# Two-layer hybrid transformer on one core: order of the second layer's projection, and the context's expert sum on TensorE

## The chip, the cores and the metric

The kernel runs on one NeuronCore of a Trainium2 chip. The metric is the device time of one execution in microseconds (us), as the median of several runs. The engines are called TensorE (PE in the rows; PEld is its loading of weights), VectorE (DVE), ScalarE (ACT), GpSimd (POOL) and SyncE (SP). In this kernel SP and GpSimd issue the transfers.

## The reference, cut to what matters

256 latent tokens and 256 context tokens of width 1024 go through two layers. Only the latents are returned, so layer 1 uses the context's h for keys and values alone.

```python
for l in range(DEPTH):                                     # DEPTH = 2
    with_ctx = l < DEPTH - 1
    mod   = (silu(c) @ w_mod[l] + b_mod[l]).reshape(B, 6, 1, 1024)     # latents
    mod_c = (silu(c_ctx) @ w_mod[l] + b_mod[l]).reshape(6, 1024)       # context
    sh1, sc1, g1, sh2, sc2, g2 = (mod[:, i] for i in range(6))
    sh1c, sc1c, g1c, sh2c, sc2c, g2c = (mod_c[i] for i in range(6))
    h  = _ln(x) * (1 + sc1) + sh1
    hc = _ln(xc) * (1 + sc1c) + sh1c
    pa, pb, pc = split(h @ w_in[l], [P_A, P_A + P_B])
    pa_c, pb_c, pc_c = split(hc @ w_in[l], [P_A, P_A + P_B])
    # three groups of heads: A grouped-query, B neighbourhood, C low-rank;
    # latents attend to latents and context, context to context only
    y = concat([y_gqa, y_na, y_mla]) @ w_out[l]
    x = _ln_affine(ALPHA * x + g1 * y, ln1_g[l], ln1_b[l])
    h = _ln(x) * (1 + sc2) + sh2
    x = _ln_affine(ALPHA * x + g2 * _hier_moe(h, ...), ln2_g[l], ln2_b[l])
    if with_ctx:                                           # layer 0 only
        ...
        xc = _ln_affine(ALPHA * xc + g2c * _hier_moe(hc, ...), ln2_g[l], ln2_b[l])
```

`_hier_moe` chooses one of 4 groups for each token, two of the 8 experts in it, and adds the two experts' outputs with weights.

## The kernel before

Tokens are worked on in four blocks of 128: blocks 0 and 1 are the latents, 2 and 3 the context. On-chip memory is managed by hand: `mem` hands out pieces of 23 units of 128 x 2048 floats, and a new piece waits for the last use of the old one at its place. All large weights come through one list, `stream`, in the order in which it was written; `pump` issues the next load while the pieces loaded and not yet dropped stay under a limit `cap`, whose values towards the end of layer 0 stand in `HC`. Plain loads are issued on SP (L161), loads of experts that are chosen at run time on GpSimd (L142). The order of the instructions on each engine is made by a planner when the kernel is built, from a priority that follows the order of the program; `high_priority` moves a block ahead, and `issue_after` puts an instruction behind another one on its engine. When the kernel runs, each engine serves its instructions in that order.

A matrix product with a large weight is made of three products (L457 to L459): `split` takes a weight apart into a high part (ScalarE, L451) and a low part (VectorE, L452), and the activations are taken apart likewise (L506 and L507).

*End of layer 0.* Passes over the experts end with a loop whose count is known only at run time (L1501); no engine carries work across it. The output rows of most experts lie in DRAM (`ys`). For each block `fetch` gathers the two rows of every token (L1482) into `ACC` and `two`. `fold` scales and adds them, multiplies by the gate g2 and adds the sum to the residual X (L1489 on ScalarE; L1491, L1492, L1493 on VectorE). `combine` adds what the last passes kept on chip, by products with one-hot matrices (L1284), multiplied by g2 (L1293). Then `deepnorm` makes the residual, its norm, and the norm of the next layer (L427 to L438, with L416 and L438 on ScalarE and L419 on GpSimd); here it runs as `second`, called `before` in layer 1.

*Start of layer 1.* `before` runs for the latents with high priority, then `rest_of` folds and combines the context's blocks, with the fold behind the latents' norm on VectorE. `fill(4)` takes four steps of the modulation's product (L320, one weight of 1 MB each). `turned` transposes the normed rows (L489), applies the modulation (L497 on ScalarE and L494 on VectorE for one column of blocks each) and takes the result apart; so h stands in `HT`. The projection follows in the order qa, cq, B chunks 0 and 1 for the latents; then the context's h; then kc (keys of A and the low-rank keys) for all four blocks, B chunks 2 to 4 for all 512 tokens, and v.

In the attention stage that follows, one further step of the modulation's product is put behind each unit of scores.

## Time and profile before

| | |
|---|---|
| median of 3 runs | 1108.3 us (1107.69 to 1109.35) |
| profiled execution | 1106.13 us |
| its span, from the first to the last instruction | 1104.2 us |
| TensorE busy | 994.6 us, 90% of the span |
| VectorE, ScalarE, GpSimd busy | 511.2, 353.1, 302.0 us |
| moved by DMA | 300.54 MB, mean 272 GB/s |

The busy share of an engine is an average over stages with different limits, so the page alone doesn't tell what a change in one stage is worth. Times in the rows count from the start of the span. A row of a timeline gives the start, the time that the merged instructions took, the engine, the line, the operation, the tiles written and read, the count, and in brackets the idle time before it with what ended it. A row of windows gives the stretch, its length, the busy time with the count of instructions of PE, PEld, DVE, ACT and POOL (or of the one engine asked for), the granted clock of TensorE as a share of 2.4 GHz, the busy share of the DMA engines and GB/s. A slice of the page is 27.6 us, a digit its busy share in tenths. An engine with a q behind its name is the engine's sequencer or queue.

### The profile page before, as it was taken

To read this page: it belongs to the slowest core of one execution; us is meant where nothing else is said; L and a number is where in the kernel's file an instruction comes from. 1 tells how busy PE (TensorE), PEld (TensorE's weight loads), DVE (VectorE), ACT (ScalarE), POOL (GpSimd) and SP (SyncE) were. 2 spreads that over 40 slices of the span, in tenths; PEclk is the share of its full clock that TensorE was granted. 3 is DMA by queue.
4 is the path that set the end of the run, shared out by engine and by line. 5 is a ranking of instruction groups with operands and counts; after the bars stand their busy time and mean duration, and the time that the engine had idled before them with its cause. 6 is when DMAs were issued, how large, how long until landed. Compare 5 with 4: busy or idle time off the path is not lost. (4 is left out here: it accounts for less than half of the span.)

```text
span 1104.2 us, 14811 instructions
## 1 busy us (share of the span) xinstructions
PE 994.6 (90%) x5525; PEld 571.6 (52%) x5525; DVE 511.2 (46%) x1364; ACT 353.1 (32%) x712; POOL 302.0 (27%) x325
## 2 busy tenths in 40 slices
PE   4999999999999999999985479999998899999894
PEld 2788745457866454444332259844466554433231
DVE  5643357775577210100013887266666654242244
ACT  4533155563552111111112365144444222111111
POOL 2111133350001432343341222042300145344420
PEclk9999999999999999999998789999997899999997
DMA  9812157610269999999998653435425799999992
GB/s 374 321 64 88 48 191 278 218 44 34 107 259 390 399 423 422 363 414 421 423 421 352 249 202 112 173 137 193 150 78 230 306 387 423 421 421 421 420 421 90
DMA packets 46207, 300.54 MB, mean 272 GB/s; under 512 B 5394, under 2 KB 5778, under 8 KB 14388
## 3 DMA queue, kind: packets, MB, share of 16 engines
q0 software_dynamic: 25824, 177.81, 39.2%
q1 hardware_dynamic: 20308, 121.75, 29.4%
q8 instruction: 45, 0.74, 0.3%
q14 instruction: 30, 0.25, 0.1%
HBM read 292.19 MB, written 7.34 MB: 271 GB/s over the span
## 5 line engine op out<-in xcount | busy, mean ns | idle before, releaser
L142 POOL DMA_INDIRECT u<-in_w_exp,u x162 | 161.1, 994 | 307.4 <-PE psa L1204 95.9
L1204 PE MATMUL psa<-u,u 128*32 128x512 f32 (+2 forms) x1040 | 212.9, 596 | 8.1 <-DMA u<-in_w_exp,u 8.1
L458 PE MATMUL psa<-u,u 128*128 128x512 f32 (+3 forms) x400 | 140.0, 351 | 2.2 <-DVE u L452 2.2
L457 PE MATMUL psa<-u,u 128*128 128x512 f32 (+3 forms) x400 | 140.8, 356 | 0.9 <-ACT u L506 0.7
L459 PE MATMUL psa<-u,u 128*128 128x512 f32 (+3 forms) x400 | 139.1, 351 | 0.1
L1204 PEld LDWEIGHTS psa<-u,u 128*32 128x32 f32 (+2 forms) x1040 | 64.6, 126 | 132.5 <-issue 109.1
L1191 PEld LDWEIGHTS psc<-u,u 128*128 128x128 f32 x640 | 83.0, 197 | 33.2 <-issue 29.0
L1191 PE MATMUL psc<-u,u 128*128 128x256 f32 x640 | 93.7, 297 | 3.0 <-DVE u L1177 2.1
L889 POOL TENSOR_SCALAR u<-u,ri 128x512 f32<-128x512 f32 (+1 forms) x48 | 68.4, 1430 | 99.1 <-DVE ri L887 81.5
L1211 DVE TENSOR_TENSOR scr<-scr,psa 128x256 f32<-128x256 f32 x26 | 10.9, 421 | 163.4 <-ACT scr L1210 157.7
L458 PEld LDWEIGHTS psa<-u,u 128*128 128x128 f32 x400 | 76.1, 190 | 12.9 <-DVE u L452 4.3
L457 PEld LDWEIGHTS psa<-u,u 128*128 128x128 f32 x400 | 75.5, 190 | 12.2 <-ACT u L506 1.1
L459 PEld LDWEIGHTS psa<-u,u 128*128 128x128 f32 x400 | 75.4, 190 | 9.3 <-issue 0.9
L886 ACT ACTIVATE u<-psa,nm 128x512 f32<-128x512 f32 (+1 forms) x96 | 58.4, 615 | 54.7 <-DVE nm L884 49.8
L1262 PE MATMUL pse<-u,scr 128*64 128x512 f32 (+1 forms) x288 | 70.4, 599 | 0.8 <-DMA u<-in_w_exp,u 0.8
L452 DVE TENSOR_TENSOR u<-u,u 128x1024 fp32r<-128x1024 f32 (+4 forms) x38 | 56.1, 1486 | 19.5 <-ACT u L451 19.4
L1210 ACT ACTIVATE scr<-psa 128x256 f32<-128x256 f32 x26 | 10.0, 385 | 171.5 <-PE psa L1204 171.5
L1193 ACT ACTIVATE u<-psc 128x512 f32<-128x512 f32 x52 | 31.1, 597 | 101.5 <-PE psc L1191 58.9
L884 DVE TENSOR_REDUCE nm<-psa 128x1 f32<-128x512 f32 (+1 forms) x80 | 53.1, 683 | 13.1 <-PE psa L874 9.5
L419 POOL TENSOR_TENSOR lns<-lns,mhalf 128x1 f32<-128x1 f32 x22 | 14.2, 648 | 162.7 <-DVE lns L418 130.3
L1249 PE MATMUL pse<-u,scr 128*32 128x512 f32 (+2 forms) x232 | 57.3, 600 | 1.4 <-ACT scr L1239 1.4
L451 ACT ACTIVATE u<-u 128x1024 fp32r<-128x1024 f32 (+4 forms) x38 | 47.4, 1266 | 16.2 <-PE psa L458 3.5
(317 smaller groups left out, 1366.5 us busy)
## 6 DMA issues: line engine op xcount, KB each, us to landing
u<-in_w_mod SPq DMA_DIRECT2D x48, 1024.0 KB, 6.5
u<-in_w_exp SPq DMA_DIRECT2D x30, 1024.0 KB, 6.9
u<-in_w_out SPq DMA_DIRECT2D x8, 1024.0 KB, 4.8
ys<-u SPq DMA_DIRECT2D x12, 512.0 KB, 8.2
u<-in_w_in_b SPq DMA_DIRECT2D x10, 512.0 KB, 11.7
u<-in_w_in_v SPq DMA_DIRECT2D x4, 960.0 KB, 5.9
u<-in_w_in_qa SPq DMA_DIRECT2D x4, 768.0 KB, 11.7
u<-in_ln_rows SPq DMA_DIRECT2D x6, 512.0 KB, 7.1
```

Source lines behind the costliest of these rows:

```text
L142: G.indirect_dma_start(out=b.ap(UNIT), out_offset=None, in_=wexp_rows, in_offset=bass.IndirectOffsetOnAxis(ap=idx, axis=0), bounds_check=N ...
L452: V.tensor_tensor(l_[:, c], w[:, c], h[:, c].bitcast(F32), OP.subtract)
L457: PE.matmul(p, lhsT=a[0], rhs=b[0], start=first, stop=False)
L458: PE.matmul(p, lhsT=a[0], rhs=b[1], start=False, stop=False)
L459: PE.matmul(p, lhsT=a[1], rhs=b[0], start=False, stop=final)
L884: V.tensor_reduce(out=nm[:, s, 0:n], in_=pv, axis=AX.X, op=OP.max, negate=True)
L886: S.activation(P[:, i, :], pv[:, i, :], AF.Exp, bias=nm[:, s, i:i + 1], accum_out=su[:, s, i:i + 1])
L889: (G if s == 0 else V).tensor_scalar(P[:, i, :], P[:, i, :], ri[:, s, i:i + 1], None, op0=OP.mult)
L1191: PE.matmul(pv[:, j, :], lhsT=H[b][:, k * 128:(k + 1) * 128], rhs=OH[:, b, :], start=(b == 0 and i == 0), stop=(b == nb - 1 and i == 1))
L1204: PE.matmul(g[r, :], lhsT=XG[:, k, at * 128 + r.start:at * 128 + r.stop], rhs=W(t, k // 4).v(4, 512)[:, k % 4, :], start=(k == 0), stop=(k ...
L1249: PE.matmul(y[r, :], lhsT=hc[:, c * 128 + r.start:c * 128 + r.stop], rhs=W(t, 2).v(2, D)[:, c, f * 512:f * 512 + 512], start=(c == 0), sto ...
L1262: PE.matmul(y[r, :], lhsT=hc[:, c * 128 + r.start:c * 128 + r.stop], rhs=W(t, 2).v(2, D)[:, c, f * 512:f * 512 + 512], start=(c == 0), sto ...
```

## The change

In layer 1, the list of loads, the filler steps and the projection are put in another order; kc is multiplied for the latents first and for the context later, with the parts of its weight kept in between (`keep`); B chunks 2 to 4 are multiplied in two halves of 256 tokens, with their weights kept likewise (`at`, `kept`). The limit on loaded pieces becomes 3 units once the latents' h is made (`HC[4]`).

In layer 0, the fold of the two context blocks is left out. Four diagonal matrices are made from the identity and the tokens' weights (`diag`), and `combine` adds the products of these with the gathered rows to the same sum on TensorE, in plain f32. The sum is copied by ScalarE, and the multiplication by g2 is done later in `second`, on VectorE behind the last part of the latents' h (`lowest`), where the norm then adds it to the residual.

```diff
-HC = (8, 7, 3, 5)
+HC = (8, 7, 3, 5, 3)
...
-    for k in ("qa", "cq"):
-        for c in range(2):
-            stream_chunk(k, 1, c)
+    for c in range(2):
+        stream_chunk("qa", 1, c)
+    stream_mod(1, 1, 0, 2)
+    for c in range(2):
+        stream_chunk("cq", 1, c)
     for c in range(2):
         stream_b(1, c)
-    stream_mod(1, 1, 0, 4)
     for c in range(2):
         stream_chunk("kc", 1, c)
     for c in range(2, 5):
         stream_b(1, c)
-    stream_mod(1, 1, 4, 8)
+    stream_mod(1, 1, 2, 4)
     for c in range(2):
         stream_chunk("v", 1, c)
+    stream_mod(1, 1, 4, 8)
...
-            V.tensor_tensor(lo, wv, hi.bitcast(F32), OP.subtract)
+            lowest.append(V.tensor_tensor(lo, wv, hi.bitcast(F32), OP.subtract).ins)
...
-        def chunk(k, blocks):
+        def chunk(k, blocks, keep=False):
...
-                pre.pop((k, c))
+                if not keep:
+                    pre.pop((k, c))
...
-        def p_b(c):
+        def p_b(c, at=None):
...
+            if c in kept:
+                w = kept.pop(c)
+            else:
+                w = split(take(("inb", l, c)), 1024)
+                drop(("inb", l, c))
+                pump()
+            if at == 0:
+                kept[c] = w
             n = 256 if (last and c < 2) else 512
+            ts = slice(0, n) if at is None else slice(256 * at, 256 * at + 256)
...
-                three(p[:, 0:n], [x[:, j, :] for x in wv], hpart(j, slice(0, n)), j == 0, j == 7)
+                three(p[:, ts], [x[:, j, :] for x in wv], hpart(j, ts), j == 0, j == 7)
...
             rest_of()
+            fill(2)
             for c in range(2):
                 presplit("qa", c)
             make_h()
-            fill(4)
             for j in range(0, 8, 2):
                 turned([(j, 0), (j + 1, 0)])
             for b in range(2):
                 xn[b].free()
+            pump(HC[4])
             together(*[before(b, xn) for b in range(2, 4)])
             p_qa()
             p_cq()
             for c in range(2):
                 p_b(c)
+            p_kc(chunk("kc", lat, True))
+            for c in range(2, 5):
+                p_b(c, 0)
+                fill(c > 2)
             for j in range(0, 8, 2):
                 turned([(j, 1), (j + 1, 1)])
...
-            p_kc(chunk("kc", every))
+            p_kc(chunk("kc", range(2, 4)))
             for c in range(2, 5):
-                p_b(c)
+                p_b(c, 1)
             p_v()
...
+                    if final and not last and b > 1:
+                        pairs += [(diag.v(2, 2, 128)[:, b - 2, j, :], r[:, fs]) for j, r in
+                                  enumerate((ACC[b], two[b].v(D)))]
...
+                    elif final and b > 1:
+                        S.activation(ACC[b][:, fs], p, AF.Copy)
...
+        diag = None if last else mem.get(512)
...
             fetch(range(2, nb))
+            for b in range(2):
+                for j in range(2):
+                    S.activation(diag.v(2, 2, 128)[:, b, j, :], ident, AF.Copy, scale=sc_[:, b + 2, 2 + j:3 + j])
...
         def second(b, xn):
             xn[b] = mem.get(D) if last else acc[b]
+            if not last and b > 1:
+                with tc.issue_after(lowest[-1]):
+                    V.tensor_tensor(ACC[b], ACC[b], BC["g2", 1], OP.mult)
...
             if not last:
-                with tc.issue_after(normed[-1]):
-                    fold(range(2, nb))
                 combine(fin, range(2, nb), True)
+                for x in two[2:] + [diag]:
+                    x.free()
```

## Rows read from the trace of the kernel before

**Rows 1.** Page, 40 slices of the span: busy tenths of TensorE:

```profile
PE   4999999999999999999985479999998899999894
```

**Rows 2.** Busy times by windows, whose columns are told in the section above:

```profile
604.00:642.60 38.60, 19.31 (x80) 10.40 (x81) 33.04 (x64) 15.90 (x23) 10.07 (x12) 0.69 0.62 214
...
677.00:722.50 45.50, 45.50 (x238) 39.35 (x237) 14.86 (x48) 10.13 (x26) 5.03 (x8) 1.00 0.31 112
...
722.50:860.00 137.50, 125.15 (x619) 70.87 (x616) 89.57 (x221) 63.91 (x132) 33.24 (x30) 0.93 0.47 166
...
900.00:1060.00 160.00, 152.79 (x850) 62.23 (x848) 57.51 (x118) 25.70 (x48) 67.26 (x68) 1.00 1.01 418
```

**Rows 3.** TensorE's waits, 604 to 690 us: line, releaser, total, times, longest:

```profile
PE pse L320 <- DMA u<-in_w_mod: 7.3, 2, 7.0
...
PE psc L680 <- DVE scr L609: 2.0, 1, 2.0
```

**Rows 4.** Timeline of TensorE between the two layers:

```profile
615.94 1.05 PE L320 MATMUL pse<-u,csil 128*32 128x512 f32 x2
...
629.52 1.54 PE L489 MATMUL psc<-ident,u 128*128 128x128 f32 x6 [1.40 <-ACT u L438]
...
638.03 3.64 PE L320 MATMUL pse<-u,csil 128*32 128x512 f32 x16 [6.97 <-DMA u<-in_w_mod]
...
641.61 1.25 PE L489 MATMUL psc<-ident,u 128*128 128x128 f32 x8
...
642.61 0.42 PE L457 MATMUL psa<-u,u 128*128 128x384 f32 x1
```

**Rows 5.** ScalarE's timeline of the same stretch:

```profile
612.96 1.15 ACT L1489 ACTIVATE u<-u,sc__2337 128x1024 f32<-128x1024 f32 x1 [5.39 <-DMA u<-ys,find]
...
615.62 1.15 ACT L1489 ACTIVATE u<-u,sc__2337 128x1024 f32<-128x1024 f32 x1 [1.51 <-DMA u<-ys,find]
...
616.68 1.13 ACT L416 ACTIVATE scr<-u,lns 128x1024 bf16<-128x1024 f32 x1
...
630.46 1.21 ACT L497 ACTIVATE scr<-psc,modT 128x256 f32<-128x256 f32 x2 [0.99 <-PE psc L489]
```

**Rows 6.** VectorE's timeline of the same stretch:

```profile
611.93 0.15 DVE L415 TENSOR_SCALAR lns<-dns 128x1 f32<-128x1 f32 x1
...
628.04 2.48 DVE L1491 SCALAR_TENSOR_TENSOR u<-u,sc__2337,u 128x1024 f32<-128x1024 f32 x2
...
630.43 2.36 DVE L1492 TENSOR_TENSOR u<-u,u 128x1024 f32<-128x1024 f32 x2
...
637.37 0.99 DVE L494 TENSOR_SCALAR scr<-psc,modT 128x256 f32<-128x256 f32 x2
...
639.41 1.30 DVE L507 TENSOR_TENSOR u<-scr,u 128x512 fp32r<-128x512 f32 x2
```

**Rows 7.** SP's timeline: issues of weight loads:

```profile
588.45 0.81 SPq L161 DMA_DIRECT2D u<-in_w_in_cq  x2
...
603.91 10.40 SPq L161 DMA_DIRECT2D u<-in_w_mod  x3
...
630.55 0.33 SPq L161 DMA_DIRECT2D u<-in_w_mod  x1
```

**Rows 8.** Last of eight gathers (L1482) on GpSimd; landing times of all:

```profile
608.01 1.33 POOL L1482 DMA_INDIRECT u<-ys,find  x1 [0.30 <-issue]
...
DMA to landing us min/median/max: 7.5/18.4/25.2
```

**Rows 9.** Windows of TensorE alone: matmuls of 256 columns, then 512:

```profile
674.70:684.17 9.47, 9.47 (x81) 1.00 0.01 2
...
684.94:689.97 5.03, 5.03 (x23) 1.00 0.00 0
```

**Rows 10.** Timeline of TensorE: a filler step, f32 products of 128x512:

```profile
651.75 1.06 PE L320 MATMUL pse<-u,csil 128*32 128x512 f32 x8 [0.34 <-DMA u<-in_w_mod]
...
726.23 2.88 PE L811 MATMUL psa<-u,u 128*128 128x512 f32 x6
```

More of the change, by code (lines that the diff above doesn't have):

```diff
@@ L419, in moments @@
         G.tensor_tensor(rs[:, 2:3], rs[:, 1:2], mhalf[:, 0:1], OP.pow)
-    normed = []
+    lowest = []
     def deepnorm(x, h, gain, bias, last=False, alpha=ALPHA, total=None, eps=EPS):
@@ L436, in deepnorm @@
                 yield
-            normed.append(V.tensor_tensor(rs[:, 0:1], rs[:, 3:4], rs[:, 2:3], OP.mult).ins)
+            V.tensor_tensor(rs[:, 0:1], rs[:, 3:4], rs[:, 2:3], OP.mult)
             S.activation(h, x, AF.Identity, bias=rs[:, 0:1], scale=rs[:, 2:3])
@@ L551, in chunk @@
                 for x in w:
-                    x.free()
+                    if not keep:
+                        x.free()
         def lead(k):
@@ L684, in p_qa @@
                 defer(turn)
-        def p_b(c):
+        kept = {}
+        def p_b(c, at=None):
             if c == 0:
@@ L691, in p_b @@
                     K.extend(x.v(n) for x in k)
-            w = split(take(("inb", l, c)), 1024)
-            drop(("inb", l, c))
-            pump()
+            if c in kept:
[6 more added lines that the diff above has]
+                kept[c] = w
             n = 256 if (last and c < 2) else 512
+            ts = slice(0, n) if at is None else slice(256 * at, 256 * at + 256)
             wv = [x.v(8, 128) for x in w]
@@ L698, in p_b @@
             for j in range(8):
-                three(p[:, 0:n], [x[:, j, :] for x in wv], hpart(j, slice(0, n)), j == 0, j == 7)
+                three(p[:, ts], [x[:, j, :] for x in wv], hpart(j, ts), j == 0, j == 7)
             if c < 2:
-                S.activation(QB[c][:, 0:n], p[:, 0:n], AF.Copy, scale=0.125)
+                S.activation(QB[c][:, ts], p[:, ts], AF.Copy, scale=0.125)
             elif c < 4:
-                S.activation(KB[c - 2], p, AF.Copy)
+                S.activation(KB[c - 2][:, ts], p[:, ts], AF.Copy)
             else:
-                S.activation(QB[2][0:64, :], p[0:64, 0:nq], AF.Copy, scale=0.125)
-                V.tensor_copy(KB[2][0:64, :], p[64:128, :])
-            for x in w:
-                x.free()
+                if at != 1:
+                    S.activation(QB[2][0:64, :], p[0:64, 0:nq], AF.Copy, scale=0.125)
+                V.tensor_copy(KB[2][0:64, ts], p[64:128, ts])
+            if at != 0:
+                for x in w:
+                    x.free()
             tick()
@@ L1592, in rest_of @@
             if not last:
-                with tc.issue_after(normed[-1]):
-                    fold(range(2, nb))
                 combine(fin, range(2, nb), True)
+                for x in two[2:] + [diag]:
+                    x.free()
             for k in list(split_y.values()) + oht:
```

## The prediction

> **What bounds the kernel now.** I read the page's slices first [rows 1]. TensorE is close to full nearly everywhere. The one deep dip inside the span lies at the 22nd to 24th digit, where layer 0 hands over to layer 1, and there the edits lie. Next come busy times by stage [rows 2]. From 604.0 to 642.6 us TensorE works 19.3 of 38.6 us. The rest of the projection (677.0 to 722.5) is wholly busy, the attention stage behind it is at 125 of 137.5 us, and the last long stage (900 to 1060) moves 418 GB/s at full DMA share. Its expert loads depend on the routing of layer 1 and on memory that attention gives back, so time saved before 720 should arrive at the end. What remains is the handover, and there the list of waits [rows 3] and the four timelines [rows 4 to 7] must be read side by side.
>
> The timeline of TensorE [rows 4] shows it empty from 617.0 (615.94 + 1.05) until the latents' normalised rows come (L489, for the second block at 629.52), then waiting 7.0 us for a weight of the modulation (L320 at 638.03, rows 3). That step ran at half speed: 16 matmuls in 3.64 us, where eight take 1.06 us at 2.4 GHz [rows 4, 10]. The projection starts at 642.61. Three different things hold it back.
> First, ScalarE. It serves its instructions in order. Two scalings of the context's expert rows (L1489) sit in front of the latents' L416 and wait for their gathers until 612.96 and 615.62 [rows 5]. The input of L416 was there at 611.93 + 0.15 = 612.1 [rows 6], yet it starts at 616.68: 4.6 us of a serial chain.
> Second, VectorE. From 628.04 to 637.37 it folds the context's rows (two instructions each of L1491, L1492, L1493, then four of L1293; the first two groups stand in rows 6). L494, which the latents' transposed h needs, comes behind them, although ScalarE's half (L497) began at 630.46 [rows 5].
> Third, SP. The fourth modulation weight is issued only at 630.55 [rows 7], and TensorE, also in order, stands before it until 638.03.
>
> **The change part by part.** The fold goes away and its sum goes to TensorE, the filler steps ahead of the latents' h shrink from four to two, and work that needs only latents moves ahead of the context's h.
>
> *ScalarE's fold out of the chain.* Without L1489 the first L416 can start at 612.1. The four small scalings of the identity wait for no DMA. Gain 4.6 us; the second block's L489 moves from 629.5 to about 624.9.
>
> *VectorE's fold and the two filler steps out of the way.* L494 then follows L497, in the old run's times at about 631.1, instead of 637.37: 6.3 us. In the old run another context sum (1.1 us) stood between L494 and L507, and L320 and the second group of transposes stood before the projection until 642.61 [rows 4, 6]. The new wait after the last L507 keeps the context's product behind all of the latents' h; what queues behind it on VectorE is only the context's own chain. In the old run's times L507 would end and the projection start at about 633.9, so 8.7 us earlier. The low bound is the 6.3 us alone. With the first part: start at 642.6 - 4.6 - 8.7 = 629.3.
>
> *Diagonal products on TensorE.* For two blocks, two halves and two operands there are eight f32 products of 128x512, each two instructions, so 16. The nearest row is L811: six such instructions in 2.8 us, 0.47 each [rows 10]; 16 take 7.5 us. They need the gathers. The last is issued at 608.0, and the quickest of the eight landed 7.5 us after its issue [rows 8]: 615.5. I take 7.5 and not the median of 18.4, because most of the eight were issued into the expert stream, and this one has no expert load behind the loop in front of it. The old work of this place ended at 617.0, so TensorE is done at 624.5, just before the L489 that can start at 624.9. I put 0.4 us on it, bounds 0 and 3.1.
>
> *The clock.* The granted clock over 604 to 642.6 was 0.69 [rows 2]. Old: the filler steps took the slow start and lost 3.64 - 2.1 = 1.5 us. New: the projection may take it. TensorE will have been idle for a shorter time, as the products fill it until 624.5. Bounds 0 and 1.5, I take 0.8.
>
> *Two filler steps moved later.* Eight instructions are one step, 1.06 us [rows 10]. Two steps now lie in a stretch where TensorE is full: +2.1 us.
>
> *B chunks in two halves.* Three chunks of 24 matmuls of 512 columns become 144 of 256. Of matmuls with 512 columns 22 begin in 5.03 us, 0.2286 each, and of those with 256 columns 79 in 9.47 us, 0.120 each [rows 9] (one and two in the counts had begun before). So 17.3 - 16.5 = +0.8 us. The keys are already multiplied block by block; splitting them by block adds nothing to TensorE, and their weights are split once and kept.
>
> *VectorE behind the start.* Two products of the context (2.36 us for two of this shape, as L1492 in rows 6) and its first sum (1.24, half of L1491's pair) now come after the latents' h and ahead of the split of the second projection weight. TensorE would wait up to 3.6 us for it; or the old wait for L609 (2.0 us, rows 3) disappears because VectorE has 9.7 us less of folding. Bounds -2.0 and +3.6, I take +1.5. That the context's h comes later costs nothing, as TensorE has the latents' keys (48 x 0.12 = 5.8 us) and half of the B chunks (8.6) to do first; without that cover up to 14 us of TensorE time would lie open. ScalarE's four copies out of PSUM take about 0.6 us each, like L497, and lie beside it.
>
> *The loads.* Two weights of the modulation now come ahead of cq, and the rest come later. Before the loop one of 1 MB takes the place of three pieces of 0.5 MB; I cost this at nothing, since SP's issues after 603.9 [rows 7] give cq about 20 us until it is needed.
>
> Sum: -4.6 - 8.7 + 0.4 + 0.8 + 2.1 + 0.8 + 1.5 = -7.7 us. On the profiled execution, 1106.1 us with a span of 1104.2, that is 1098.4. That execution lies 2.2 us under the median of 1108.3, so the forecast for the median is 1100.6.
>
> **Rivals.** *Copies in ScalarE's queue.* The new copies of the context's sums wait for the products, until about 624.5. If they stand ahead of the latents' L438, ScalarE again blocks the chain as L1489 did, and the first 4.6 us are lost: -3.1, so 1105.2. For it: exactly this happened in rows 5. Against: they now come behind two more steps, and the latents' chain has the higher priority.
> *The modulation weight still late.* The change moves the wait and doesn't remove it: the two later filler steps stand in TensorE's queue between the B chunks, and their weights are loaded only under the smaller limit on loaded pieces, three units. The price is the 7.0 us of rows 3 once more: -0.7, so 1107.6. Against: the step lies some 25 us behind the start.
> *Gathers late, slower than before.* TensorE now waits for the gathers in front of the latents' transposes; before, only the folds did. About 3 us lie between landing and need. Each further us is a us lost; a landing 10.7 us late (at 626) eats the gain, and over 13 us late makes it slower than now by more than can be told from no change. The largest landing time of the eight is 25.2 us [rows 8]: 633.2, 17.7 us late, which gives -7.7 + 17.7 - 3 = +7.0, so 1115.3. It decides where SP's longer list of loads starts at 603.9 beside them. Against it: in the old run three weights of 1 MB were issued from 603.9 on as well, and that gather came in 7.5 us.
> The Trainium skill (DMA: Bandwidth & Descriptors, "Queues, rings and completion order") says that each DMA engine takes turns, packet by packet, between the queue rows that have work. By that rule a longer list on SP's queue does not put the gathers further back; only expert loads ahead of them in their own queue would, and by it this rival gives no more than the forecast's time. The fast landing after the loop agrees, 7.5 us against the largest of 25.2 us; no run yet shows the longer list.
>
> **How the numbers follow.** Forecast 0.62, copies 0.14, late weight 0.12, late gathers 0.12. A measurement of this kernel can tell about 0.2%, 2.2 us, from no change. Faster: 0.62 + 0.14 = 0.76; same: 0.12; slower: 0.12. The predicted time is the forecast's, 1100.6. With every open bound on its good side (0 for the products and the clock, -2.0 for VectorE) it is -12.4, about 1096; I set the low end at 1095.5. The high end takes in the late weight, 1108.0; beyond it lie the late gathers.
>
> **What would show it.** Right: no L1489 for the context; the first L416 by 613; L494 within a us of its L497; the projection's first matmul between 628 and 632, no wait of 7 us for a modulation weight; the end of the projection some 7 us earlier than 722.5, and the stages behind it as long as before. The products' step is wrong if TensorE waits long for the gathers before L489; VectorE's if waits for L452 or L609 of more than 4 us stand in the projection; the cover if TensorE waits before the context's transposes. The prediction as a whole is wrong if the projection starts early and attention or the last DMA stage takes the gain back.

## The result, and the profile after

The changed kernel takes 1114.9 us, the median of 7 runs (1113.5 to 1119.3), against 1108.2 us for the kernel before in runs beside it. The ratio is 1.0066 with a 95% interval of 1.0050 to 1.0082: about 7 us slower. The forecast was 1100.6 in a range that ended at 1108.0. The profiled execution took 1114.92 us with a span of 1113.1, against 1106.13 and 1104.2. Two stray executions (1966.5 us of `e7_keys_only` below, 2458.3 us of the kernel before beside e5 to e8) are left out of every ratio and of e7's median.

Lines moved with the edit. In the changed kernel `split` is L453 (ScalarE) and L454 (VectorE), the products of the projection L459 to L461, the filler step L322, the norm's L416 to L440 stand two lines lower than before, the transposes are L491, the modulation L499 and L496, `combine` L1306, ScalarE's new copies of the context's sums L1315, and the context's product with g2 L1616. The heads' norm and rotation (L603 to L609 before) are L607 to L613.

Busy times by stage of the changed kernel, with the columns of [rows 2]: handover from the first product of `combine` to the first matmul of the projection, projection, attention to its last values, and from there to the ranks of the routing:

```profile
605.50:638.20 32.70, 24.27 (x77) 13.13 (x77) 20.96 (x56) 14.14 (x23) 9.98 (x12) 0.82 0.62 227
638.20:727.80 89.60, 84.31 (x541) 76.92 (x540) 50.32 (x116) 38.28 (x75) 15.33 (x16) 0.93 0.39 139
727.80:817.70 89.90, 86.58 (x457) 39.78 (x456) 58.64 (x137) 43.13 (x102) 30.94 (x26) 1.00 0.50 172
817.70:867.90 50.20, 40.04 (x170) 31.14 (x169) 30.92 (x81) 20.93 (x31) 2.21 (x4) 0.77 0.48 183
```

The same four stages of the kernel before:

```profile
604.50:642.60 38.10, 19.28 (x80) 10.38 (x81) 32.83 (x62) 15.73 (x23) 10.07 (x12) 0.69 0.62 217
642.60:722.80 80.20, 77.06 (x464) 67.22 (x463) 43.98 (x114) 35.92 (x71) 14.92 (x16) 1.00 0.45 164
722.80:811.70 88.90, 85.63 (x444) 39.79 (x442) 58.26 (x137) 43.85 (x102) 31.03 (x26) 1.00 0.46 157
811.70:859.40 47.70, 38.96 (x172) 30.71 (x171) 30.95 (x81) 20.06 (x31) 2.21 (x4) 0.80 0.47 181
```

The handover became 5.4 us shorter. The projection behind it became 9.4 us longer, attention 1.0 and the stage behind it 2.5. What remains to the end of the span is 245 us in both. So two questions stand: why the handover gained 5.4 us and not 13.3 (642.6 to 629.3), and what makes the projection longer.

**The handover.** ScalarE's timeline of the changed kernel:

```profile
614.85 1.15 ACT L418 ACTIVATE scr<-u,lns 128x1024 bf16<-128x1024 f32 x1 [7.86 <-DVE lns L417]
...
623.12 0.60 ACT L1315 ACTIVATE u<-psa 128x512 f32<-128x512 f32 x1 [7.02 <-PE psa L1306]
624.83 0.60 ACT L1315 ACTIVATE u<-psa 128x512 f32<-128x512 f32 x1 [1.12 <-PE psa L1306]
625.33 1.14 ACT L418 ACTIVATE scr<-u,lns 128x1024 bf16<-128x1024 f32 x1
```

VectorE's timeline of the same stretch (the two L417 give the inputs of the two L418):

```profile
607.03 0.09 DVE L1437 MEMSET capv<- 128x2 f32 x2 [2.08 <-ACT u L453]
607.06 1.23 DVE L1518 TENSOR_TENSOR u<-u,u 128x1024 f32<-128x1024 f32 x1
...
614.67 0.15 DVE L417 TENSOR_SCALAR lns<-dns 128x1 f32<-128x1 f32 x1
...
618.39 0.15 DVE L417 TENSOR_SCALAR lns<-dns 128x1 f32<-128x1 f32 x1
...
636.82 1.18 DVE L496 TENSOR_SCALAR scr<-psc,modT 128x256 f32<-128x256 f32 x2 [0.35 <-ACT scr L499]
...
642.19 2.35 DVE L1616 TENSOR_TENSOR u<-u,u 128x1024 f32<-128x1024 f32 x2
```

And TensorE's timeline:

```profile
615.14 1.06 PE L322 MATMUL pse<-u,csil 128*32 128x512 f32 x6
619.52 10.56 PE L1306 MATMUL psa<-u,u 128*128 128x512 f32 x24 [3.33 <-DMA u<-ys,find]
634.06 0.69 PE L491 MATMUL psc<-ident,u 128*128 128x128 f32 x2 [3.98 <-ACT u L440]
...
638.18 0.67 PE L459 MATMUL psa<-u,u 128*128 128x384 f32 x1
```

The first L418 starts the moment its input is there. The second block's input is there at 618.5 and L418 starts at 625.33: 6.8 us behind two copies that wait for the products. This is the first rival of the prediction, in the trace. The products themselves wait 3.3 us for the gathers and then take 10.6 us, until 630.1 and not 624.5. VectorE's step came as predicted: L496 starts as soon as ScalarE's L499 releases its buffer, after 0.35 us of waiting (in [rows 6] it stood behind the fold), and no wait for a modulation weight is left in front of the projection.

**The projection.** TensorE's waits, 604 to 728 us, in the columns of [rows 3]:

```profile
...
PE psa L460 <- DVE u L454: 2.8, 2, 1.8
PE psa L459 <- DVE scr L607: 1.4, 1, 1.4
PE psa L461 <- DVE u L454: 1.1, 1, 1.1
...
```

The first of the splits that it waits for, of the second projection weight (cq), on VectorE:

```profile
649.46 1.22 DVE L454 TENSOR_TENSOR u<-u,u 128x1024 fp32r<-128x1024 f32 x1
```

Windows inside the projection (the fourth column from the right is POOL's, then the granted clock):

```profile
638.20:643.00 4.80, 4.80 (x18) 4.72 (x17) 4.34 (x7) 2.80 (x5) 0.00 (x0) 0.50 0.00 0
...
652.00:656.60 4.60, 2.75 (x23) 2.55 (x22) 3.75 (x13) 4.45 (x7) 2.55 (x2) 1.00 0.01 2
656.60:660.00 3.40, 3.40 (x19) 3.38 (x17) 2.27 (x8) 1.69 (x3) 2.05 (x3) 0.54 0.00 0
660.00:664.00 4.00, 1.51 (x8) 0.92 (x7) 3.13 (x7) 2.10 (x4) 0.84 (x2) 0.93 0.74 262
664.00:666.90 2.90, 2.90 (x15) 2.90 (x15) 2.46 (x6) 1.42 (x3) 1.93 (x1) 0.50 0.02 6
```

TensorE now begins the projection before cq is split. The context's product (L1616), its sums and its norm stand in VectorE's queue in front of these splits (L454), and TensorE waits for them. It was idle 5.3 us (89.60 - 84.31) instead of 3.1. Three stretches run at half clock, 1.2 GHz: 638.2 to 643, 656.6 to 660, 664 to 666.9, together some 5.4 us of work lost (half of 4.8, 46% of 3.4, half of 2.9). TensorE had waited ahead of each of them, but a gap alone does not decide it: behind the wait of 0.95 us at 650.7 the clock stayed at 1.00, and the projection before was at 1.00 throughout with a wait of 2.0 us in it (L680, [rows 3]).

### The profile page after: what moved, and what is told of

Same layout as the page of the kernel before. It is cut to its first block, busy times and chain, and to the rows that moved or that the text cites. A ratio compares the mean times of both kernels' runs of the same rounds, so it can differ in the third digit from the quotient of the medians.

```text
span 1113.1 us, 14992 instructions
## 1 busy us (share of the span) xinstructions
PE 1008.9 (91%) x5613; PEld 587.9 (53%) x5613; DVE 506.3 (45%) x1357; ACT 354.8 (32%) x720; POOL 303.5 (27%) x325
## 5 line engine op out<-in xcount | busy, mean ns | idle before, releaser
L459 PE MATMUL psa<-u,u 128*128 128x256 f32 (+3 forms) x424 | 149.0, 354 | 4.0 <-ACT u L453 1.7
L460 PE MATMUL psa<-u,u 128*128 128x256 f32 (+3 forms) x424 | 147.2, 348 | 4.7 <-DVE u L454 4.7
L461 PE MATMUL psa<-u,u 128*128 128x256 f32 (+3 forms) x424 | 145.5, 347 | 1.2 <-DVE u L454 1.1
L459 PEld LDWEIGHTS psa<-u,u 128*128 128x128 f32 x424 | 83.1, 197 | 16.3 <-ACT u L453 3.4
L460 PEld LDWEIGHTS psa<-u,u 128*128 128x128 f32 x424 | 83.4, 197 | 13.6 <-DVE u L454 5.8
L461 PEld LDWEIGHTS psa<-u,u 128*128 128x128 f32 x424 | 82.5, 196 | 9.8 <-DVE u L454 1.4
L1281 PE MATMUL pse<-u,scr 128*64 128x512 f32 (+1 forms) x288 | 67.2, 600 | 1.0 <-DMA u<-in_w_exp,u 0.6
L454 DVE TENSOR_TENSOR u<-u,u 128x1024 fp32r<-128x1024 f32 (+4 forms) x38 | 56.3, 1486 | 23.3 <-ACT u L453 23.0
L1306 PE MATMUL psa<-u,u 128*128 128x512 f32 x144 | 48.4, 470 | 11.9 <-DVEq L1526 4.5
```

The costliest lines, as they stand in the source:

```text
L454: V.tensor_tensor(l_[:, c], w[:, c], h[:, c].bitcast(F32), OP.subtract)
L459: PE.matmul(p, lhsT=a[0], rhs=b[0], start=first, stop=False)
L460: PE.matmul(p, lhsT=a[0], rhs=b[1], start=False, stop=False)
L461: PE.matmul(p, lhsT=a[1], rhs=b[0], start=False, stop=final)
L1281: PE.matmul(y[r, :], lhsT=hc[:, c * 128 + r.start:c * 128 + r.stop], rhs=W(t, 2).v(2, D)[:, c, f * 512:f * 512 + 512], start=(c == 0), sto ...
```

## The experiments

Two theories stood at the start. A: the copies in ScalarE's queue hold the chain, as in rival 1, and without them the change pays. B: the sum on TensorE pays, and the new order (loads, filler steps, projection) costs. One table holds all runs: each ratio is against runs of the kernel before beside it, and 0.001 is 1.1 us. The stages are those of the windows above, from one profiled execution each, cut at the same instructions. They leave out what lies ahead of `combine`, whose first product began at 604.5 us before, at 605.5 in the changed kernel, and anywhere from 604.3 to 609.1 in the others (e1 at 608.3 and e9 at 604.3, which differ up to there in the list of loads alone). So the stages of one execution do not add up to a ratio.

| kernel | median, us | ratio, 95% interval | handover | projection | attention | to the ranks |
|---|---|---|---|---|---|---|
| before | 1108.2 | 1 | 38.1 | 80.2 | 88.9 | 47.7 |
| after | 1114.92 | 1.0066 [1.0050, 1.0082] | 32.7 | 89.6 | 89.9 | 50.2 |
| e1_sum_only | 1098.47 | 0.9914 [0.9891, 0.9936] | 30.0 | 81.5 | 87.0 | 46.2 |
| e2_order_only | 1114.34 | 1.0056 [1.0034, 1.0078] | 39.1 | 82.9 | 89.9 | 49.3 |
| e3_copies_behind | 1117.25 | 1.0079 [1.0054, 1.0103] | 36.1 | 88.7 | 89.9 | 50.3 |
| e4_diag_late | 1108.73 | 1.0005 [0.9988, 1.0021] | 33.4 | 84.5 | 89.9 | 46.1 |
| e5_copies_diag | 1111.19 | 1.0016 [1.0002, 1.0029] | 31.4 | 87.2 | 89.9 | 49.4 |
| e6_sum_copies | 1098.82 | 0.9904 [0.9882, 0.9926] | 28.5 | 82.1 | 86.9 | 49.3 |
| e7_keys_only | 1107.94 | 0.9987 [0.9974, 1.0000] | 30.0 | 91.8 | 85.7 | 46.1 |
| e8_loads_only | 1106.35 | 0.9976 [0.9964, 0.9988] | 31.7 | 82.8 | 89.4 | 46.2 |
| e9_steps_only | 1101.69 | 0.9952 [0.9933, 0.9970] | 29.5 | 81.9 | 88.9 | 47.7 |
| e10_whole_chunks | 1112.78 | 1.0049 [1.0033, 1.0066] | 33.4 | 89.7 | 88.9 | 47.6 |
| e11_steps_early | 1111.25 | 1.0035 [1.0019, 1.0051] | 35.0 | 85.5 | 88.9 | 47.7 |
| e12_split_behind | 1106.70 | 0.9983 [0.9964, 1.0001] | 29.6 | 85.8 | 89.9 | 49.4 |

A difference of two kernels below is the difference of their ratios times 1108 us, with the intervals' half widths added as squares (the root of their sum).

### The two halves of the change, each alone

`e1_sum_only` is the kernel before with the context's sum on TensorE (`diag` allocated where it is first used), and nothing of the order:

```diff
-                with tc.issue_after(normed[-1]):
-                    fold(range(2, nb))
                 combine(fin, range(2, nb), True)
+                for x in two[2:] + [diag]:
+                    x.free()
```

with the edits of `combine`, `second` and the diagonal matrices as in the change.

> The kernel before with the context's sum on TensorE alone (diag allocated at its first use); loads, filler steps and projection as before. Theory A (the copies out of PSUM in ScalarE's queue hold up the latents' chain, the order of the projection is sound): the latents' last norm ends at about 634, not 629.5, but L494 no longer waits for a fold and TensorE waits for the modulation weight until 638 as before, so the projection starts at 642 to 644: 1108 to 1110 us. Theory B (the new order of loads and projection is what costs, the sum gains): the projection starts by 640 and the time is 1104 to 1107 us.

`e2_order_only` is the reverse: `HC`, the list of loads, `fill`, `keep` and `at` as in the change; `rest_of` stays as it was:

```diff
             if not last:
                 with tc.issue_after(normed[-1]):
                     fold(range(2, nb))
                 combine(fin, range(2, nb), True)
```

> The changed kernel with the old fold of the context on ScalarE and VectorE; loads, filler steps and projection in the new order. Theory A: the latents' norm ends at 629 to 631 as before, L494 waits for the fold until 637, and without two filler steps the projection starts at 639 to 641; waits behind it as in the changed kernel, so 1107 to 1111 us. Theory B: the waits for splits and the half clock in the projection (some 8 us) come with the order, 1112 to 1116 us.

Measured: the sum alone gains 9.5 us, a ratio of 0.9914, and is the fastest form so far; the order alone loses 6.2. Theory B has the direction; e1 is better than either theory expected. The time of e2 lies in B's range, but B's mechanism does not show there: its projection is only 2.7 us longer than before, with 0.5 us of waiting for a split and a clock of 0.98, so the waits and the half clock of the changed kernel's projection did not come with the order alone. The handover of e1, 30.0 us, is 8.1 shorter than before, and its projection stays at full clock:

```profile
608.30:638.30 30.00, 26.12 (x95) 13.71 (x96) 21.68 (x56) 15.80 (x26) 10.09 (x12) 0.85 0.77 278
638.30:719.80 81.50, 77.96 (x465) 67.48 (x464) 48.38 (x113) 35.50 (x71) 15.33 (x16) 1.00 0.43 160
```

Against [rows 2] TensorE has 26 us of work in the handover instead of 19: the products, and still four filler steps (32 instructions). The granted clock over the handover is 0.85 instead of 0.69, and the projection starts at full clock.

### The copies, and what stands behind them

`e3_copies_behind` is the changed kernel with the copies behind the latents' last normalisation:

```diff
-            S.activation(h, x, AF.Identity, bias=rs[:, 0:1], scale=rs[:, 2:3])
+            normed.append(S.activation(h, x, AF.Identity, bias=rs[:, 0:1], scale=rs[:, 2:3]).ins)
...
-                        S.activation(ACC[b][:, fs], p, AF.Copy)
+                        with tc.issue_after(normed[-1]):
+                            S.activation(ACC[b][:, fs], p, AF.Copy)
```

> The changed kernel with the four copies out of PSUM put behind the latents' last norm activation on ScalarE. Theory A: the first L418 of the second block starts at about 618.5 instead of 625.3; the norm ends 6 us earlier, and then the products on TensorE, until 630, hold the transposes: the projection starts at 633 to 635, and the time falls by 3 to 5 us to 1110 to 1112. Theory B: the projection starts earlier but waits for splits and loads instead, 1114 to 1116 us.

Measured: 1117.25, no gain. ScalarE's timeline of e3 says why:

```profile
622.12 1.15 ACT L418 ACTIVATE u<-u,lns 128x1024 f32<-128x1024 f32 x1 [1.72 <-DVE lns L417]
...
632.31 1.67 ACT L453 ACTIVATE u<-u 128x512 fp32r<-128x512 f32 x3 [8.95 <-PE psa L1306]
633.89 1.13 ACT L418 ACTIVATE u<-u,lns 128x1024 f32<-128x1024 f32 x1
```

Another instruction took the copies' place: the split of the second piece of qa's weight, whose memory the products give back. It waits 8.95 us for them, and block 1's L418 stands behind it.

`e4_diag_late` is the changed kernel with `diag` allocated where it is first used, so that the last passes run without its quarter of a unit being held:

```diff
         two = []
-        diag = None if last else mem.get(512)
...
             fetch(range(2, nb))
+            diag = mem.get(512)
```

> The changed kernel with the piece for the diagonal matrices taken at its first use instead of ahead of the passes. If this piece, by moving others in memory, costs only the wait for g2 in the last passes (7.8 us of TensorE's wait, given back to 1.0 us at the loop): 1113.5 to 1114.5 us, cq loaded at 625 as now. If the placement also makes the loads of cq late (issued at 624.8 and 630.1), these move to about 606 and the time falls by 3 to 6 us, 1109 to 1112.

`e5_copies_diag` has both edits, that of e3 and that of e4.

> The changed kernel with two edits together: the diagonal's piece is taken at first use (as in e4_diag_late), and ScalarE's copies of the context's sums stand behind the latents' last normalisation. Theory A (the copies in ScalarE's queue cost the latents' chain some 4 us, once no other wait stands there): 1104 to 1106, 3 to 5 us under e4_diag_late. Theory B (the copies are not what ends last, or the split of the first weight waits for the products in their place, as in e3_copies_behind): 1108 to 1111, with the second L453 behind a wait for L1306 of several us.

Measured: `diag` taken late gains 6.8 us (+-2.5) against the changed kernel, and 7.0 (+-3.1) with the copies moved (e5 against e3). The allocation of one quarter unit was no part of the prediction at all. Neither expectation for e4 came as told: cq was still issued late (626.1 and 631.4 us), and yet the time fell just below both ranges. Moving the copies again brings nothing, e5 against e4 +1.2 (+-2.4). VectorE's timeline of e5:

```profile
626.81 0.16 DVE L439 TENSOR_TENSOR lns<-lns 128x1 f32<-128x1 f32 x1 [0.32 <-POOL lns L421]
631.59 1.90 DVE L454 TENSOR_TENSOR u<-u,u 128x512 fp32r<-128x512 f32 x3 [4.61 <-PE psa L1306]
...
634.21 0.16 DVE L439 TENSOR_TENSOR lns<-lns 128x1 f32<-128x1 f32 x1 [0.62 <-POOL lns L421]
```

ScalarE's half of the split now found other memory, VectorE's half did not: 4.6 us of waiting for the products, ahead of block 1's L439. `e12_split_behind` is e5 with these three pieces behind that L439:

```diff
-            V.tensor_tensor(l_[:, c], w[:, c], h[:, c].bitcast(F32), OP.subtract)
+            with tc.issue_after(behind) if behind else nullcontext():
+                V.tensor_tensor(l_[:, c], w[:, c], h[:, c].bitcast(F32), OP.subtract)
```

where `behind` is the latents' last L439 for qa's second piece, and nothing otherwise.

> e5_copies_diag with VectorE's three split pieces of the first weight's second chunk put behind the latents' last L439. In e5_copies_diag these pieces waited 4.61 us for the products L1306, and block 1's L439 stood behind them until 634.21. If that in-order wait is what holds the handover: L439 by 630, the projection 3 to 4 us earlier against the start of combine (27.5 to 28.5 us instead of 31.4), 1106 to 1108. If the projection's first 25 us go at the pace of VectorE and an earlier start is given back there: the start moves and the projection grows by as much, 1109.5 to 1112.

Measured: 1106.7, and e12 is 3.7 us (+-2.5) faster than e5. The lines of e12 that answer to those of e5 (L440 and L456 here):

```profile
628.11 0.16 DVE L440 TENSOR_TENSOR lns<-lns 128x1 f32<-128x1 f32 x1 [0.66 <-POOL lns L422]
630.71 1.90 DVE L456 TENSOR_TENSOR u<-u,u 128x512 fp32r<-128x512 f32 x3 [2.44 <-PE psa L1309]
```

So the in-order wait was real, and it stood in three places one after the other: ScalarE's copies, ScalarE's split, VectorE's split. Only with the last of them gone does the time move, by 1 to 6 us against e5. Against e4, where none of the three was touched, e12 gains 2.4 us (+-2.7), which can't be told from nothing. Even then e12 stays 7.6 us (+-3.2) behind e1, so the queues are not the main loss.

`e6_sum_copies` is e1 with the copies behind the latents' last normalisation, by the edit of e3:

```diff
-                        S.activation(ACC[b][:, fs], p, AF.Copy)
+                        with tc.issue_after(normed[-1]):
+                            S.activation(ACC[b][:, fs], p, AF.Copy)
```

> e1_sum_only (the context's sum on TensorE, all else as before) with the copies behind the latents' last normalisation on ScalarE. In e1_sum_only all six split pieces of the first weight ran at 608.3, ahead of the products, so no split can wait for them; the second block's L416 had its input at 619.7 and started at 623.85 behind the copies. Theory A: 4 us off the chain, projection start 26 to 27 us after the start of combine instead of 30, 1094 to 1096. Rival (TensorE's filler steps or VectorE end as late as the chain did): 1097 to 1100, no difference to e1_sum_only.

Measured: as e1 (-1.1 +-3.5). ScalarE's timeline of e6:

```profile
628.02 1.24 ACT L438 ACTIVATE u<-u,lns 128x1024 f32<-128x1024 f32 x1 [0.85 <-DVE lns L437]
629.17 2.04 ACT L1297 ACTIVATE u<-psa 128x512 f32<-128x512 f32 x4
631.08 1.04 ACT L497 ACTIVATE scr<-psc,modT 128x256 f32<-128x256 f32 x2
```

The chain up to L438 became shorter, but the four copies now stand in front of L497, 2.0 us, and the projection's start moved 1.5 us against the start of `combine`. In the medians it can't be told from nothing. Theory A fell as a cause of the result: the waits are there, the price is small.

### What in the new order costs

Four kernels take the order apart, all with the sum on TensorE and `diag` taken late. `e7_keys_only` adds to e1 the latents' keys ahead of the context's h:

```diff
             for c in range(2):
                 p_b(c)
+            p_kc(chunk("kc", lat, True))
             for j in range(0, 8, 2):
                 turned([(j, 1), (j + 1, 1)])
...
-            p_kc(chunk("kc", every))
+            p_kc(chunk("kc", range(2, 4)))
```

> e1_sum_only plus one part of the new order of the projection: the keys (kc) are multiplied for the latents ahead of the context's h, with the weight's parts kept; the list of loads, the filler steps and the whole B chunks stay as before. If the order of the loads and filler steps costs the 10 us between e1_sum_only and e4_diag_late: 1097 to 1100. If the order of the projection costs them: 1103 to 1108.

`e8_loads_only` adds to e1 the change's list of loads, `pump(HC[4])`, `fill(2)` ahead of the latents' h and `fill(c > 2)` behind the whole B chunks:

```diff
             rest_of()
+            fill(2)
...
             make_h()
-            fill(4)
...
+            pump(HC[4])
             together(*[before(b, xn) for b in range(2, 4)])
...
                 p_b(c)
+                fill(c > 2)
```

> e1_sum_only plus the new list of loads, the limit of three units and the filler steps in their new places (two ahead of the latents' h, two behind B chunks 3 and 4), with the old order of the projection. If the loads and filler steps cost the 10 us between e1_sum_only and e4_diag_late: 1103 to 1108, with a wait of TensorE for a modulation weight or for cq, and two more steps behind the scores. If the order of the projection costs them: 1097 to 1101.

`e9_steps_only` moves only the steps and their weights:

```diff
-    stream_mod(1, 1, 0, 4)
+    stream_mod(1, 1, 0, 2)
...
+    stream_mod(1, 1, 2, 4)
     for c in range(2):
         stream_chunk("v", 1, c)
+    stream_mod(1, 1, 4, 8)
...
-            fill(4)
+            fill(2)
...
                 p_b(c)
+                fill(c > 2)
```

> e1_sum_only with two of the four filler steps taken out of the stretch ahead of the projection and put behind B chunks 3 and 4, and their two weights of the modulation put behind the B chunks in the list; the rest of the list, the limits and the order of the projection stay as before. If the place of the steps makes most of the 8 us between e1_sum_only and e8_loads_only: 1103 to 1106, with a wait for the modulation's weight behind the B chunks and some 2 us more in the attention stage. If the longer list ahead of cq and the limit of three units make it: 1098 to 1101.

`e10_whole_chunks` is e4 with the B chunks 2 to 4 whole again, behind the context's h:

```diff
-            for c in range(2, 5):
-                p_b(c, 0)
-                fill(c > 2)
...
-                p_b(c, 1)
+                p_b(c)
+                fill(c > 2)
```

> e4_diag_late with B chunks 2 to 4 whole again and behind the context's h; the latents' keys stay ahead of it, the loads and filler steps as in the change. If the halves cover the making of the context's h, as the prediction took it: 1111 to 1115, with a wait of TensorE for the context's L496 of 5 us or more, as e7_keys_only had (5.3 us). If the halves cost more than they cover: 1105 to 1108, under e4_diag_late.

`e11_steps_early` is e4 with all four steps ahead of the latents' h and their four weights ahead of cq:

```diff
-    stream_mod(1, 1, 0, 2)
+    stream_mod(1, 1, 0, 4)
...
-    stream_mod(1, 1, 2, 4)
...
-            fill(2)
+            fill(4)
...
                 p_b(c, 0)
-                fill(c > 2)
```

> e4_diag_late with all four filler steps ahead of the latents' h, as in the kernel before, and all four of their weights ahead of cq in the list; none between the B chunks. If the place of the two steps is what costs in the new order: 1103 to 1106, without the wait of 3.5 us for a modulation weight and with some 2 us less in the attention stage. If cq, now four weights of the modulation further back, comes too late: 1109 to 1113, with a wait of TensorE for cq or its split behind qa.

Measured against e1: the two steps moved cost 4.2 us (+-3.2), steps and loads together 6.9 (+-2.8), which leaves 2.7 (+-2.4) for the longer list, the limit and the place of the first two steps; the latents' keys ahead cost 8.1 (+-2.9). Keys and loads together (e10) cost 15.0 (+-3.1), the sum of the two. The halves give 4.9 (+-2.6) of it back (e4 against e10, which also takes the two late steps behind the context's h); keys and halves together cost 3.2 (+-2.3), e4 against e8. So e4 stands 10.1 (+-3.1) behind e1. For e9 neither expectation held alone; it lies between.

TensorE's longest wait in the projection of e7:

```profile
PE psc L489 <- DVE scr L494: 5.3, 1, 5.3
```

and two of e10, 604 to 735 us:

```profile
PE psc L491 <- DVE scr L496: 6.0, 2, 4.9
...
PE pse L322 <- DMA u<-in_w_mod: 3.2, 1, 3.2
```

ScalarE's timeline of e7, the first modulation of the context's h:

```profile
679.39 0.56 ACT L497 ACTIVATE scr<-psc,modT 128x256 f32<-128x256 f32 x1 [5.60 <-DVE scr L611]
```

The context's first transposes were done at 673.5 (TensorE's L489 began at 672.43 and took 1.04). But L497 writes into one of the rotating scratch buffers, and waits 5.6 us until VectorE's L611, the end of the keys' norm and rotation, gives it back; TensorE in turn waits 5.3 us. The projection's mean clock is 0.96, that is 3.7 us of its 91.8. Another 1.9 of the 91.8 are filler steps (14 instructions more than e1 has there), which the attention stage is spared. Before, these keys came behind the context's h and nothing waited for them. The halves fill exactly this hole: in e4 and in the changed kernel TensorE waits for nothing in front of the context's transposes.

In e11 the steps' wait is gone (e4 had 3.5 us for that weight), but the total is 3.3 us (+-2.5) worse than e4. The time lies in the range expected for a late cq (issued at 627.6 and 632.9, in [rows 7] at 588.5), but no engine waits for cq in e11. TensorE's longest wait in its projection is another:

```profile
PE psa L458 <- DVE scr L606: 3.9, 1, 3.9
```

In e11 the products also wait longer for the gathers (3.7 us), the handover is 35.0 instead of 33.4, and half of ScalarE's split of qa stands behind the products (from 631.2 us on), as in the changed kernel. So e11 does not show that the late cq is what costs.

## Why the prediction failed

Of the signs that I named, the first L418 came at 614.85 and not by 613, the projection started at 638.2 and not between 628 and 632, and it ended at 727.8 and not some 7 us before 722.5. Step by step:

**What bounds the kernel, and that a gain before 720 arrives at the end:** right. From the ranks to the end it is 244 to 247 us in every kernel.

**ScalarE's fold out of the chain, -4.6.** Half right. The first L418 waited for nothing but its input, which came at 614.8 and not at 612.1: VectorE took up the latents' fold behind the loop (L1518) at 607.06, after a wait of 2.1 us for ScalarE's split; before, the same instruction began at 604.33. Only the two kernels that take `diag` early (the changed one and e3) have this wait. In e1 the first L416 starts 7.7 us behind the first product of `combine`, before 12.2: there the 4.6 us were gained. The second block lost 6.8 us again to the copies. I had this as a rival at 0.14 and 4.6 us, and argued against it from priority; in-order queues decided it.

**VectorE's fold out of the way, -8.7.** The mechanism was right (L496 right behind L499, no weight waited for), and together with the first part e1 shows its size: the handover 8.1 us shorter, 9.5 us in the whole. My sum for these two with the products and the clock was -12.1, and with VectorE behind the start, which is in e1 too, -10.6.

**Diagonal products, +0.4 within 0 to 3.1.** Mis-sized. I counted 16 instructions, but the eight one-hot products of the same four sums come behind the same wait: 24, at 0.44 us each 10.6 us. GpSimd's gathers behind the loop (count, shortest, median and longest issue in ns, first and last start):

```profile
L1507 POOL DMA_INDIRECT u<-ys,find x3: 988/989/1802, 606.1 to 609.8; - x3
```

The last gather was issued at 609.8, 1.8 us later than in [rows 8], and TensorE was released at 619.5, 9.7 us after it and not 7.5. They ended at 630.1, 5.6 us past my 624.5. The slack that I gave the gathers, about 3 us, is 1.9 by the prediction's own figures (624.9 - 7.5 - 615.5). The rival of late gathers had the right place and a far too large price; that its 1115.3 lies beside the measured 1114.9 is chance.

The runs show what the longer list does to the gathers. From the issue of the last one to TensorE's release it takes 7.5 to 7.7 us in the four kernels that load cq early as before (e1, e6, e7, e9) and 9.8 to 11.9 us in the eight with a longer list ahead of it (the changed one, e3, e4, e5, e8, e10, e11, e12). The Trainium skill (DMA: Bandwidth & Descriptors, "Queues, rings and completion order") has each DMA engine take turns, packet by packet, between the queue rows that have work. That fits the size, 2 to 4 us and not 17.7, and in the changed kernel two queues moved 1.91 and 1.31 MB side by side from 612 to 620 us; but my inference from it, that a longer list leaves the gathers where they were, was wrong.

**The clock, +0.8 within 0 to 1.5.** Too small. The first 4.8 us of the projection at half clock cost 2.4, and I priced no second or third fall behind the waits inside the projection (3.0 us more).

**Two filler steps later, +2.1.** Low, if anything: e9 measures 4.2 (+-3.2), and 2.1 lies in that interval. What I left out is that the two steps, when they come late, can also wait for their weight: 2.8 us in e8 and 3.5 in e4 (rival two, at half its price), nothing visible in the changed kernel, where TensorE waited for VectorE meanwhile.

**Keys for the latents first, nothing; B chunks in halves, +0.8.** I priced the matmuls of the keys (none added) and forgot the norm and the rotation that follow them, a chain over three engines, which now ends ahead of the context's h and holds a scratch buffer that h needs: 8.1 us in e7, without the halves. The halves are worth -4.9, being the cover. I saw the cover (5.8 and 8.6 us of TensorE work) but credited it to the keys as well. In the change both stand together: 3.2 us (+-2.3) instead of 0.8.

**VectorE behind the start, +1.5 within -2.0 to 3.6.** In the changed kernel it looks beyond the bound: 5.3 us of waits, four and not one, and the half clock behind them. But e1 and e4 have the same product, sums and norm in VectorE's queue, and TensorE waits for no split there. So this order alone does not cost the waits; they come with the memory, below.

**The loads, nothing.** 2.7 us (+-2.4) in e8 against e9. Part of it is the later gathers, above. cq was issued at 624.83 and 630.1 instead of 588.5; an engine is seen waiting for it in two kernels, ScalarE in e2 (3.5 us) and e12 (2.0).

**Not in the sum at all:** the memory. `diag` held early costs 6.8 us (+-2.5). Its first effect is in the last passes: TensorE's waits of the changed kernel, 560 to 605 us, against 0.6 us in the kernel before:

```profile
PE psc L392 <- ACT u L394: 7.8, 1, 7.8
```

ScalarE's copy of g2's rows (L394) there waits for stores of expert rows (`ys`) to leave the memory that it was given. At the start of `combine` nothing of it is left (605.5 us against 606.8 in e4), since other waits of the passes vanish beside it. Its second effect is in the splits. Behind the loop ScalarE splits all six pieces of qa in e4, but three in the changed kernel, the others from 630.61 on, behind the products. Then cq, whose first split ScalarE makes ahead of the context's work in e4 and TensorE's product of qa (L460) holds up in the changed kernel; first e4, then the changed kernel:

```profile
635.82 1.04 ACT L453 ACTIVATE u<-u 128x1024 fp32r<-128x1024 f32 x1
...
645.25 2.01 ACT L453 ACTIVATE u<-u 128x1024 fp32r<-128x1024 f32 x2 [3.70 <-PE psa L460]
```

VectorE's half of that split follows at 636.89 in e4 and at 649.46 in the changed kernel, behind L1616, the sums and the norm. TensorE's waits for L454 in the projection are 3.9 us in the changed kernel and 3.0 in e3, which both take `diag` early, and at most 0.9 in every other kernel. e4, in its profiled execution, gains in the projection (5.1) and in the stage behind attention (4.1), most of it as granted clock: 0.97 of 84.5 us instead of 0.93 of 89.6, and 0.82 of 46.1 instead of 0.77 of 50.2. The other executions agree: the mean clock of the whole execution was 0.960 to 0.963 in all seven of the changed kernel and 0.965 to 0.971 in all ten of e4, between the medians 0.6% of some 1000 us of TensorE work, so about 6 us (an estimate). Which buffer's place leads to which fall of the clock is open.

The sum, then: the part on TensorE is worth -9.5 (+-2.5), where I had -10.6 (-4.6 - 8.7 + 0.4 + 0.8 + 1.5), so this part held as a whole; the order costs 10.1 (+-3.1) on top of it, where I had 2.9 (steps and loads 6.9 for 2.1, keys and halves 3.2 for 0.8); and the early `diag` another 6.8 (+-2.5), where I had nothing. These last two are the steps that failed. -9.5 + 10.1 + 6.8 = +7.4, the measured +7.3 (the three are steps along one path from before to after, so they must add up; each is a measured step).

The version to keep is e1: the context's sum on TensorE with the old order, 0.9914 [0.9891, 0.9936] of the kernel before (e6 can't be told from it).

## What to carry to other kernels

When products move ahead of other work, price everything that follows them on the other engines (norm, rotation, splits), for it takes its place in those queues too, and a start that is earlier than the engine feeding it can be given back as waits and half clock. Filler work is worth most where the engine is idle anyway. Of each new buffer ask from when it is held and whose release a later instruction then waits for; such a wait shows up under the name of an engine that has nothing to do with the data.

## What the runs showed of the hardware

The stage behind attention does the same work in all kernels and took 46.1 to 50.3 us; its mean granted clock was 0.85 in e1, 0.80 before and 0.77 in the changed kernel. In the changed kernel a wait for ScalarE's split stands ahead of the fall:

```profile
820.85 1.65 PE L459 MATMUL psa<-u,u 128*128 128x512 f32 x3 [1.72 <-ACT u L453]
```

In e6 the clock was 0.78 and TensorE had no such wait, so that wait is not the only cause; what else decides it stays open. Executions of one kernel differ too: of 17 of the kernel before, beside e9 to e11, the fastest took 1104.25 us at a mean clock of 0.967 and the slowest 1110.45 at 0.959. So a single profiled execution can lie some us beside the median, which is why the parts above are priced by ratios.
